# A decoder layer on one core: first B and A operands of the second MLP product loaded earlier, their order pinned, operands placed alike

## The chip, the cores and the metric

One core of a Trainium2 chip runs the whole kernel. The metric is the device time in microseconds (us), median of the runs; lower is better.

## What is computed

One decoder layer for a sequence of 1024 tokens and width 1024, float32 in and out. What matters here is its last part:

```python
x = x + gt1[:, None, :] * (merged @ w_out[l])
h2 = _modulate(x, norm2_g[l], sh2, sc2)
ff_out = jnp.square(jax.nn.relu(h2 @ w_ff1[l])) @ w_ff2[l]
x = x + gt2[:, None, :] * ff_out
...
return _rmsnorm(x, final_g)
```

`w_ff1` is 1024 x 4096 and `w_ff2` 4096 x 1024. Ahead of it stand a token mixing of two branches (a delta-rule recurrence and an attention with a forget gate), their gates and the projection `w_out`.

## The kernel before

Every float32 product is made of three products of rounded halves: an operand is cast to a high part on ACT, and DVE subtracts that from the operand to give the low part. Both MLP products are cut in 2 x 2 blocks and done in Strassen's way, with 7 block products instead of 8: some operands are sums of blocks (S1 to S4 on one side, T1 to T4 on the other).

**The way up** (`w_ff1`) runs over 16 pairs of column tiles. A pair has 7 products of 12 matmuls, each 128x512, in PSUM banks x, y and z. Its results, the A operands of the way down, are written to DRAM (`f_d`) by POOL's queue (`f_put`). In the last pair the first step of the way down is already mixed between the products, with operands that were loaded ahead (da and db, line 1405).

**The way down** (`w_ff2`) has 4 groups of 7 steps, given by the list `STEPS`; a step is 48 matmuls (line 1221) and sums up in the banks x or y. The steps of group 0 are numbered 0 to 6 in the text. A step needs two operands:

- the A operand dA: 1 MB from `f_d` on SP's queue (`load_a`, line 1503), ACT's two casts to dh (`hi_halves`, line 1410), DVE's two subtractions to fl (line 1591);
- the B operand: a raw block of 1 MB (`load_b`, line 1509), scaled by gt2 on DVE (`scale_b`, line 1517), for some steps a sum T of blocks (lines 1527 to 1536), then `split`: ACT's cast to wh (line 1099) and DVE's subtraction to wl (line 1100).

Step 0 takes A12 and B21, step 1 A11 and B11, step 2 S1 and T1 (from B12 and B11), step 3 S2 and T2 (from B22 and T1). After a step, the banks are added to acc by DVE (lines 1553 and 1559) or copied by ACT (line 1557).

**What sets the order.** Each engine runs its instructions in order, and so does SP with its loads. The order in which they stand is made by the framework's scheduler from the program and its estimates of time; the kernel writes the steps, and the scheduler moves instructions between them. A tile with a tag has a fixed number of buffers, so a new tile waits until the last reader of the old one is done: dA1 to dA27 take turns in the tags ar0, ar1 and dr, B21 lies in ur. B11_0 and B12_0 and the tiles of dA1 and dA2 lie where operands of the way up lay, so that a load into them waits for the last product with those.

Of the kernel before, what the change touches and what calls it, by code (L numbers as in the profile page):

```python
# [2 lines left out]

# [5 lines left out]
F32 = mybir.dt.float32  # L9
# [26 lines left out]
def build(ctx, tc, A, out):  # L36
# [6 lines left out]
    def pool(**kw):  # L43
        if kw.get("space") != bass.MemoryType.DRAM:
            kw["reuse_waits"] = "tile"
        return tc.tile_pool(**kw)
# [10 lines left out]
    def psum_pools(**banks):  # L57
        ppx.close()
        pools.clear()
        for tag, (n, size) in banks.items():  # L60
            pools[tag] = ppx.enter_context(pool(name=f"ps_{tag}", bufs=n, space=PSUM)), size

    def big(name, tag="pp"):
        return pools[tag][0].tile([P, pools[tag][1]], F32, tag=tag, name=name)
# [944 lines left out]
    gt2 = dpp.tile([P, D], F32, name="gt2")  # L1009
    sc2 = dpp.tile([P, KT], F32, name="sc2")  # L1010
    sh2 = dpp.tile([P, KT], F32, name="sh2")

    def ada_rest(gp):
        for j, dst in ((2, gt1), (5, gt2), (4, sc2), (3, sh2)):
# [82 lines left out]

    def split(hi, lo, src):
        ACT.copy(hi, src)  # L1099
        DVE.tensor_tensor(lo, src, f32(hi), ALU.subtract)  # L1100

    raw1, first, sums, rest = {}, {}, {}, {}

# [49 lines left out]
    ssq = px.tile([P, 8], F32, name="ssq2")  # L1153
    rs2 = px.tile([P, 8], F32, name="rs2")
    rtmp2 = px.tile([P, 16], F32, name="rtmp2")
    x1s = []

    def turn(t0, k, tag):
# [245 lines left out]
            nx[x] = dpr.tile([P, 4, 512], F32, name=f"d{x}0", tag=tag, bufs=1)  # L1404
            SP.dma_start(nx[x], src)

    def hi_halves(s, src):
        hs = [wp.tile([P, 2, 512], F32R, name=f"dh{s}_{i}", tag=("whi", "wlo")[s % 2], bufs=2) for i in range(2)]
        for i in range(2):
            ACT.copy(hs[i], src[:, 2 * i : 2 * i + 2])  # L1410
        return hs
# [14 lines left out]
    for j in range(2, NPAIR):  # L1426
# [33 lines left out]
        if not last:  # L1460
            rest_split(j + 1, "A22")
            first_first(j + 1)
            first_out(j + 1, 1)
    for name in ("S1", "S2", "S4"):
        f_sum(NPAIR - 1, name)
    for stack in (hx[2], hx[0], dax, hx[1], mix):
        stack.close()


    psum_pools(x=(4, 512), y=(4, 512))  # L1470
    with pool(name="fr", bufs=1, side="right") as fr, pool(name="fp", bufs=1) as fp:
        raws = {"B21": nx["b"]}
        acc = []
        ssq = fp.tile([P, 16], F32, name="ssq3")
        rs3 = fp.tile([P, 8], F32, name="rs3")
        rtmp = fp.tile([P, 16], F32, name="rtmp3")
        x1ts = {}

        STEPS = [
            ("y", True, "A12", "B21", [(0, 0)]),  # L1480
            ("x", True, "A11", "B11", [(0, 0)]),
            ("y", True, "S1", "T1", [(1, 1)]),
            ("x", False, "S2", "T2", [(0, 1)]),
            ("y", False, "S4", "B22", [(0, 1)]),
            ("x", False, "S3", "T3", [(1, 1)]),
            ("x", False, "A22", "T4", [(1, 0)]),
        ]
        flat = [(g, i) for g in range(NG) for i in range(7)]
        A_, ops, banks = {}, {}, {}

        def new_a(s):
            x = (s - 1) % 3
            A_[s] = (fr if x < 2 else dpr).tile([P, 4, 512], F32, name=f"dA{s}", tag=("ar0", "ar1", "dr")[x], bufs=1)

        def new_b(g, name):
            to, tag = {"B11": (fr, "B11"), "B12": (fr, "B12"), "B21": (dpr, "ur"), "B22": (fp, "B22")}[name]
            raws[name] = to.tile([P, 4, 512], F32, name=f"{name}_{g}", tag=tag, bufs=1)

        def load_a(s):
            g, i = flat[s]  # L1500
            if s > 2:
                new_a(s)
            SP.dma_start(A_[s], f_d[AOPS.index(STEPS[i][2]), 4 * g : 4 * g + 4].rearrange("j p n -> p j n"))

        def load_b(g, name):
            n, d = {"B11": (0, 0), "B12": (0, 1), "B21": (1, 0), "B22": (1, 1)}[name]
            if g or name not in ("B11", "B12"):
                new_b(g, name)
            SP.dma_start(raws[name], ff2[:, 8 * g : 8 * g + 8].rearrange("p (j i) n -> p j i n", i=2)[:, :, n, 512 * d : 512 * d + 512])

        new_a(2)
        new_b(0, "B12")
        new_a(1)
        new_b(0, "B11")

        def scale_b(name):
            DVE.tensor_tensor(raws[name], raws[name], by_gt2(int(name[2]) - 1), ALU.mult)

        def down_b(g, i):

            R = raws
            if i == 1:
                scale_b("B11")
            elif i == 2:
                scale_b("B12")
                R["T"] = fp.tile([P, 4, 512], F32, name=f"T_{g}", tag="T", bufs=1)
                DVE.tensor_tensor(R["T"], R["B12"], R["B11"], ALU.subtract)
            elif i == 3:
                scale_b("B22")
                DVE.tensor_tensor(R["T"], R["B22"], R["T"], ALU.subtract)  # L1530
            elif i == 5:
                DVE.tensor_tensor(R["B12"], R["B22"], R["B12"], ALU.subtract)
            elif i == 6:
                if g == 0:
                    scale_b("B21")
                DVE.tensor_tensor(R["T"], R["B21"], R["T"], ALU.subtract)
            elif i == 0:
                scale_b("B21")
            src = R[("B21", "B11", "T", "T", "B22", "B12", "T")[i]]
            if g == 0 and i == 1:  # L1540
                fr.tile([P, D], F32, name="fr_rest")
            h_, l_ = [to.tile([P, 4, 512], F32R, name=f"w{x}{g}_{i}", tag=f"w{x}", bufs=2) for x, to in (("h", fr), ("l", fp))]
            split(h_, l_, src)
            return [(h_[:, j], l_[:, j]) for j in range(4)]

        seen = set()

        def evict(o, t, d, scaled):
            sl = slice(512 * d, 512 * d + 512)
            if t >= len(acc):  # L1550
                acc.extend(fp.tile([P, D], F32, name=f"acc{t_}") for t_ in range(len(acc), t + 1))
            if (t, d) in seen:
                DVE.tensor_tensor(acc[t][:, sl], o, acc[t][:, sl], ALU.add)
            else:
                seen.add((t, d))
                if scaled:
                    ACT.copy(acc[t][:, sl], o)
                else:
                    DVE.tensor_tensor(acc[t][:, sl], o, gt2[:, sl], ALU.mult)
# [22 lines left out]
        def prepare(s):  # L1582
            if s >= len(flat):
                return
            g, i = flat[s]
            src = A_.pop(s)
            hs = hi_halves(s, src)
            fl = fp.tile([P, 4, 512], F32R, name=f"fl{s}", tag="fl", bufs=2)
            for i_ in range(2):
                sl = slice(2 * i_, 2 * i_ + 2)  # L1590
                DVE.tensor_tensor(fl[:, sl], src[:, sl], f32(hs[i_]), ALU.subtract)  # L1591
            ops[s] = [(hs[j // 2][:, j % 2], fl[:, j]) for j in range(4)], down_b(g, i)

        def loads(s):

            if s >= len(flat):
                return
            g, i = flat[s]
            load_a(s)
            if i in BL:  # L1600
                load_b(g, BL[i])

        ops[0] = nx["A"], nx["B"]
        loads(1)
        loads(2)
        for s, (g, i) in enumerate(flat):
            loads(s + 3)
            prepare(s + 1)
            if i == 5 and g + 1 < NG:
                load_b(g + 1, "B21")  # L1610
            if g == NG - 1 and i == 0:
                fg = dpp.tile([P, D], F32, name="fg", tag="gt1", bufs=1)
                POOL.dma_start(fg, A["final_g"].rearrange("(o n) -> o n", o=1).broadcast_to([P, D]))
            tag, opens, _, _, to = STEPS[i]
            fa, wb = ops.pop(s)
            for t in range(4):
                ts_ = slice(t * P, t * P + P)
                if opens:
                    banks[tag, t] = bank(f"{tag}{g}_{i}_{t}", tag)
                o = banks[tag, t]  # L1620
                for j in range(4):
                    (fh, fl), (wh, wl) = fa[j], wb[j]
                    mmx(o, fh[:, ts_], wh, opens and j == 0, False)
                    mmx(o, fl[:, ts_], wh, False, False)
                    mmx(o, fh[:, ts_], wl, False, j == 3)
                for half, d in to:
                    evict(o, t + 4 * half, d, s > 0)
                if g == NG - 1:
                    if i == 1:
                        square(t, 0)  # L1630
                    elif i == 4:
                        square(t, 1)
                        finish(t)
                    elif i == 5:
                        square(t + 4, 1)
                    elif i == 6:
                        square(t + 4, 0)
                        finish(t + 4)
            if g in (1, 2) and i >= 3:
                residual(4 * (g - 1) + i - 3)  # L1640

# [22 lines left out]
```

## Time and profile before

| | |
|---|---|
| median of 3 runs | 1678.47 us (1678.31 to 1679.96) |
| the profiled execution, its own time | 1680.21 us |
| its span in the trace | 1678.5 us |
| mean granted TensorE clock | 0.991 |
| busy: PE, DVE, ACT, POOL | 95%, 67%, 44%, 21% of the span |
| way up (first x product to last A22) | about 1022 to 1351 us |
| way down, step 1 to the last product | 1369.54 to 1661.4 us |

Times in the trace are counted from the span's start. A matmul's duration in the trace is longer than the spacing of two, since they overlap; the pace is read from start to start, or from a piece of the chain of so many matmuls.

### The profile page before, as it was taken

Reading aid. Unit: us, or ns where it says so; the run is one execution under the profiler, and the core shown is the slowest. Engines: PE = TensorE matmul, PEld = TensorE weight load, DVE = VectorE, ACT = ScalarE, POOL = GpSimd, SP = SyncE. Lnnn points to the kernel's source line nnn. Section 1 sums busy time; section 2 is a strip of 40 time slices with the busy share of each in tenths; the row PEclk is TensorE's granted clock in tenths of the full one; section 3 lists DMA queues with packets and bytes.
Section 4 is the critical chain, followed back from the end, with each engine's and each line's share of the span. In section 5 each row is a group of like instructions: output and inputs, shape, how many; then the busy total and the mean of one; then the engine's idle time right before and its main releaser. Section 6 shows DMA issues by size and latency. Waiting matters only on the chain.

```text
span 1678.5 us, 21911 instructions
## 1 busy us (share of the span) xinstructions
PE 1591.5 (95%) x8293; PEld 1274.8 (76%) x8293; DVE 1132.0 (67%) x1685; ACT 730.7 (44%) x1138; POOL 357.9 (21%) x362
## 2 busy tenths in 40 slices
PE   2989999999999999999999999999999979999997
PEld 1767777777777878888887787777777858888886
DVE  5777665657655736665737656975555579899978
ACT  5455343535454623332333234655545534433334
POOL 4310000899990011221110000122211110000000
PEclk9999999999999999999999999999999989999999
DMA  8525456422223178778767431344444474364422
GB/s 242 149 79 161 127 152 155 113 63 63 70 60 117 32 213 262 231 242 230 239 207 237 152 113 51 139 150 154 144 160 150 158 288 161 120 220 158 168 75 101
DMA packets 217111, 256.24 MB, mean 153 GB/s; under 512 B 30097, under 2 KB 156330, under 8 KB 216878
## 3 DMA queue, kind: packets, MB, share of 16 engines
q1 hardware_dynamic: 204094, 209.99, 41.3%
q0 software_dynamic: 12704, 44.57, 6.9%
q8 instruction: 65, 1.06, 0.3%
q14 instruction: 40, 0.33, 0.1%
q10 hardware_dynamic: 208, 0.28, 0.0%
HBM read 178.16 MB, written 72.45 MB: 149 GB/s over the span
## 4 chain that ended last, share of the span: by engine, by line
PE 70%; DVE 10%; DMA 7%; ACT 5%; issue 3%; SPq 0%; DVEq 0%; ACTq 0%
PE x L1221 18%; PE y L1221 11%; PE p_gb L41 5%; PE p_out L41 5%; PE p_ga L41 3%; PE p_ob L41 2%; PE p_fv L41 2%; DMA ur<-in_w_ff 2%; PE my L41 2%; PE p_fk L41 2%; PE p_fq L41 2%; PE z L1221 2%; PE p_v L41 2%; PE yv L41 2%; PE tp L825 2%
## 5 line engine op out<-in xcount | busy, mean ns | idle before, releaser
L1410 ACT CAST dh<-dA 128x1024 fp32r<-128x1024 f32 x54 | 56.4, 1046 | 139.9 <-PE x L1221 72.2
L1221 PE MATMUL x<-wh,dh 128*128 128x512 f32 x256 | 102.1, 399 | 9.4 <-ACT wh L1099 9.4
L645 POOL TENSOR_TENSOR dg<-dg,inv 128x62 f32<-128x62 f32 (+30 forms) x62 | 100.2, 1616 | 4.8
L1221 PE MATMUL x<-wl,dh 128*128 128x512 f32 x256 | 100.9, 395 | 0.0
L1221 PE MATMUL x<-wh,fl 128*128 128x512 f32 x256 | 100.1, 391 | 0.0
L644 POOL TENSOR_TENSOR inv<-dg 128x62 f32<-128x62 f32 (+30 forms) x62 | 92.8, 1497 | 4.9
L1591 DVE TENSOR_TENSOR fl<-dA,dh 128x1024 fp32r<-128x1024 f32 x54 | 65.1, 1218 | 16.1 <-ACT dh L1410 10.3
L1221 PE MATMUL y<-wh,dh 128*128 128x512 f32 x176 | 69.4, 394 | 0.0
L1221 PE MATMUL y<-wl,dh 128*128 128x512 f32 x176 | 68.6, 393 | 0.5 <-DVE wl L1100 0.5
L1221 PE MATMUL y<-wh,fl 128*128 128x512 f32 x176 | 68.3, 388 | 0.0
L829 DVE TENSOR_TENSOR pl<-tp,ph 128x512 fp32r<-128x512 f32 (+1 forms) x80 | 49.1, 631 | 24.9 <-ACT ph L828 24.6
L1221 PEld LDWEIGHTS x<-wh,dh 128*128 128x128 f32 x256 | 48.8, 191 | 19.6 <-ACT wh L1099 9.8
L885 DVE CUSTOM_DVE_ANT_0 pt<-s,cb 128x512 f32<-128x512 f32 (+2 forms) x64 | 36.4, 584 | 37.5 <-PE s L41 36.6
L887 ACT ACTIVATE pt<-pt,sm 128x128 f32<-128x128 f32 (+3 forms) x64 | 49.5, 775 | 24.4 <-DVE sm L885 23.4
L707 POOL TENSOR_TENSOR sw<-sbd,wcs 64x256 f32<-64x256 f32 x28 | 22.9, 816 | 167.9 <-DVE sbd L708 137.7
L1245 ACT ACTIVATE ff<-ff 128x512 f32<-128x512 f32 x48 | 30.3, 632 | 64.9 <-DVE ff L1331 29.5
L1221 PEld LDWEIGHTS x<-wl,dh 128*128 128x128 f32 x256 | 48.3, 189 | 12.0 <-DVE wl L1100 0.5
L1221 PEld LDWEIGHTS x<-wh,fl 128*128 128x128 f32 x256 | 48.6, 190 | 10.7
L828 ACT CAST ph<-tp 128x512 fp32r<-128x512 f32 (+1 forms) x80 | 41.6, 543 | 29.1 <-PE tp L825 27.2
L1236 POOL DMA_DIRECT2D f_d<-ff x48 | 25.9, 540 | 125.5 <-ACT ff L1246 121.1
L825 PE MATMUL tp<-ident,pt 128*128 128x128 f32 x288 | 49.6, 282 | 2.1 <-ACT pt L887 1.7
L41 PE MATMUL p_out<-h_wo,hhi 128*128 128x512 f32 x128 | 50.8, 397 | 0.6 <-ACT h_wo L1056 0.6
(586 smaller groups left out, 4932.6 us busy)
## 6 DMA issues: line engine op xcount, KB each, us to landing
dA<-f_d SPq DMA_DIRECT2D x27, 1024.0 KB
aw<-in_w_ada SPq DMA_DIRECT2D x32, 512.0 KB
ur<-in_w_ff SPq DMA_DIRECT2D x30, 512.0 KB
B<-in_w_ff SPq DMA_DIRECT2D x15, 1024.0 KB
f_d<-ff POOLq DMA_DIRECT2D x48, 256.0 KB, 4.3
wa<-in_w_ada SPq DMA_DIRECT2D x16, 512.0 KB
sc_d<-scb SPq DMA_DIRECT2D x16, 512.0 KB
sct<-sc_d SPq DMA_DIRECT2D x16, 512.0 KB
```

Source lines behind the costliest of these rows:

```text
L41: PE.matmul(o, l, r, start=start, stop=stop)
L644: POOL.tensor_tensor(tv, dg[:, 0:s, s : s + 1].broadcast_to([P, s, m]), dg[:, s : s + 1, s + 1 :].broadcast_to([P, s, m]), ALU.mult)
L645: POOL.tensor_tensor(dg[:, 0:s, s + 1 :], dg[:, 0:s, s + 1 :], tv, ALU.add)
L825: PE.transpose(tp[:, x * P : (x + 1) * P], pr[b][:, t * P : (t + 1) * P], ident)
L828: ACT.copy(ph[:, 0:w_], tp[:, 0:w_])
L829: DVE.tensor_tensor(pl[:, 0:w_], tp[:, 0:w_], ph[:, 0:w_].bitcast(F32), ALU.subtract)
L885: DVE.tensor_tensor_reduce(pt[:, c0:c1], sv, cb[:, c0:c1], -0.125, low, ALU.add, ALU.min, st_[:, x : x + 1])
L887: ACT.activation(pt[:, 0:n], pt[:, 0:n], AF.Exp, bias=low, scale=-1.0, accum_out=ls[:, b : b + 1])
L1221: PE.matmul(o, l, r, start=start, stop=stop, skip_group_check=True)
L1245: ACT.activation(f, f, AF.Relu)
L1410: ACT.copy(hs[i], src[:, 2 * i : 2 * i + 2])
L1591: DVE.tensor_tensor(fl[:, sl], src[:, sl], f32(hs[i_]), ALU.subtract)
```

## The change

It does three things.

1. *Early loads.* The code that makes the first tiles of the way down now stands ahead of the last sums of the last pair. SP loads B11 and dA1 right behind db, and DVE scales B11 at once. Step 1's high parts get buffers of their own (`wh_second`; `dh_second`, which lies in the tag dr, where dA3 lay), so that they can be made before step 0 is over. The loads of steps 1 to 3 are kept in the order in which they are written (`in_order`).
2. *Order of evictions.* `behind(done)` lets what is written under it be issued only after the last instruction in a list: the last f sums behind B11's scaling, step 0's later evictions and the preparing of steps 2 to 6 behind the low parts made before them.
3. *Three unused tiles*, `dpp_rest` (64 bytes in each partition), `px_rest` (384) and `fp_rest` (352). Nothing reads or writes them. They move what is allocated after them: before, hhi, hlo, dh and the halves of ur began at an offset of 352 within 512 bytes, S1 to S4, T1, T4, wh and h_wo0 to h_wo3 at 416, h_wo4 to h_wo7 at 480, wl and fl at 0; after the change all of these begin at 352.

```diff
+    def behind(done):
+
+        return tc.issue_after(done[-1].ins) if done else nullcontext()
...
+    dpp.tile([P, 16], F32, name="dpp_rest")
...
+    px.tile([P, 96], F32, name="px_rest")
...
-    def hi_halves(s, src):
-        hs = [wp.tile([P, 2, 512], F32R, name=f"dh{s}_{i}", tag=("whi", "wlo")[s % 2], bufs=2) for i in range(2)]
+    def hi_halves(s, src, second=False):
+        if second:
+            h = dpr.tile([P, 4, 512], F32R, name="dh_second", tag="dr", bufs=1)
+            hs = [h[:, 2 * i : 2 * i + 2] for i in range(2)]
+        else:
+            hs = [wp.tile([P, 2, 512], F32R, name=f"dh{s}_{i}", tag=("whi", "wlo")[s % 2], bufs=2) for i in range(2)]
...
+    def in_order(load, yes):
+        if yes:
+            tc.keep_in_program_order(load)
...
+    new_a(2)
+    new_b(0, "B12")
+    new_a(1)
+    new_b(0, "B11")
+    load_b(0, "B11")
+    load_a(1)
+    early = [scale_b("B11")]
+    with behind(early):
+        for name in ("S1", "S2", "S4"):
+            f_sum(NPAIR - 1, name)
...
+        fp.tile([P, 88], F32, name="fp_rest")
...
             if i == 1:
-                scale_b("B11")
+                if g:
+                    scale_b("B11")
...
-            h_, l_ = [to.tile([P, 4, 512], F32R, name=f"w{x}{g}_{i}", tag=f"w{x}", bufs=2) for x, to in (("h", fr), ("l", fp))]
-            split(h_, l_, src)
+            if g == 0 and i == 1:
+                h_ = fq.tile([P, 4, 512], F32R, name="wh_second")
+            else:
+                h_ = fr.tile([P, 4, 512], F32R, name=f"wh{g}_{i}", tag="wh", bufs=2)
+            l_ = fp.tile([P, 4, 512], F32R, name=f"wl{g}_{i}", tag="wl", bufs=2)
+            early.append(split(h_, l_, src))
...
+            if i in BL and s == 3:
+                load_b(g, BL[i])
             load_a(s)
-            if i in BL:
+            if i in BL and s != 3:
                 load_b(g, BL[i])
...
         ops[0] = nx["A"], nx["B"]
-        loads(1)
         loads(2)
         for s, (g, i) in enumerate(flat):
-            loads(s + 3)
-            prepare(s + 1)
+            if s:
+                loads(s + 3)
+            with behind(early if 0 < s < 6 else []):
+                prepare(s + 1)
...
-                for half, d in to:
-                    evict(o, t + 4 * half, d, s > 0)
+                with behind(early if s == 0 and t else []):
+                    for half, d in to:
+                        evict(o, t + 4 * half, d, s > 0)
...
+            if s == 0:
+                loads(3)
```

Two engines' rows show what moves. In the names, dA and B carry a buffer's number and not the step's. First SP's loads, from db on. Before, dA_11639 is dA3, B_0_11641 is B22, dA_11633 dA1, B_0_11634 B11, dA_11631 dA2 and B_0_11632 B12:

```order
L1405 DMA db_11488<-in_w_ff 128x4x512
L1503 DMA dA_11639<-f_d 128x4x512
L1509 DMA B_0_11641<-in_w_ff 128x4x512
L1503 DMA dA_11633<-f_d 128x4x512
L1509 DMA B_0_11634<-in_w_ff 128x4x512
L1503 DMA dA_11631<-f_d 128x4x512
L1509 DMA B_0_11632<-in_w_ff 128x4x512
L1503 DMA dA_11716<-f_d 128x4x512
L1503 DMA dA_11788<-f_d 128x4x512
```

After, B_0_11611 is B11, dA_11610 dA1, dA_11608 dA2, B_0_11609 B12, B_0_11718 B22, dA_11722 dA4, dA_11794 dA5 and dA_11720 dA3:

```order
L1411 DMA db_11490<-in_w_ff 128x4x512
L1514 DMA B_0_11611<-in_w_ff 128x4x512
L1508 DMA dA_11610<-f_d 128x4x512
L1508 DMA dA_11608<-f_d 128x4x512
L1514 DMA B_0_11609<-in_w_ff 128x4x512
L1514 DMA B_0_11718<-in_w_ff 128x4x512
L1508 DMA dA_11722<-f_d 128x4x512
L1508 DMA dA_11794<-f_d 128x4x512
L1508 DMA dA_11720<-f_d 128x4x512
```

B11 and dA1 came fourth and fifth among the rows from db on and are now the first two behind it. dA3, which came first, now comes last, behind dA4 and dA5. The wait that goes with B11's load is for the last product of the way up that reads T1l; the one with dA3's is for the last matmul of step 1, which reads dh_second.

Then DVE, from the last dl of db to the first evictions of step 0 and what makes step 1's operands. Before:

```order
L1331 TENSOR_TENSOR ff_15_11522<-y_11490,ff_15_11522 128x512
L1421 TENSOR_TENSOR dl_11569<-db_11488,dh_0_11573 128x512
L1517 TENSOR_TENSOR db_11488<-db_11488,gt_5349 128x2048
L1321 TENSOR_TENSOR ff_15_11503<-x_11469,ff_15_11503 128x512
...
L1559 TENSOR_TENSOR acc_11714<-y_0_3_11701,gt_5349 128x512
L1517 TENSOR_TENSOR B_0_11641<-B_0_11641,gt_5349 128x2048
L1591 TENSOR_TENSOR fl_11647<-dA_11633,dh_0_11643 128x1024
L1591 TENSOR_TENSOR fl_11647<-dA_11633,dh_1_11644 128x1024
L1517 TENSOR_TENSOR B_0_11634<-B_0_11634,gt_5349 128x2048
L1100 TENSOR_TENSOR wl_1_11653<-B_0_11634,wh_1_11652 128x2048
```

And after the change:

```order
L1431 TENSOR_TENSOR dl_11571<-db_11490,dh_0_11575 128x512
L1351 TENSOR_TENSOR fs_11583<-ff_15_11442,ff_15_11524 128x512
L1327 TENSOR_TENSOR ff_15_11505<-x_11471,ff_15_11505 128x512
L1517 TENSOR_TENSOR B_0_11611<-B_0_11611,gt_5349 128x2048
...
L1105 TENSOR_TENSOR wl_1_11655<-B_0_11611,wh_second 128x2048
L1622 TENSOR_TENSOR fl_11650<-dA_11610,dh_second 128x1024 x2
L1590 TENSOR_TENSOR acc_11671<-y_0_0_11658,gt_5349 128x512
L1590 TENSOR_TENSOR acc_11686<-y_0_1_11673,gt_5349 128x512
```

The scaling of db (as B21) has left this place for the time of step 6's operand. B11's scaling, wl and fl of step 1 stood behind the evictions of step 0 and now stand ahead of them, with f sums of the last pair between.

One more place, DVE between step 1's evictions and step 3's low part, after the change (T_11732 is T, x_1_3 the last bank of step 1):

```order
L1584 TENSOR_TENSOR acc_11716<-x_1_3_11780,acc_11716 128x512
L1105 TENSOR_TENSOR wl_2_11735<-T_11732,wh_2_11734 128x2048
L1517 TENSOR_TENSOR B_0_11718<-B_0_11718,gt_5349 128x2048
L1622 TENSOR_TENSOR fl_11800<-dA_11720,dh_0_11796 128x1024
L1622 TENSOR_TENSOR fl_11800<-dA_11720,dh_1_11797 128x1024
L1556 TENSOR_TENSOR T_11732<-B_0_11718,T_11732 128x2048
L1517 TENSOR_TENSOR B_1_12002<-B_1_12002,gt_5349 128x2048
L1105 TENSOR_TENSOR wl_3_11806<-T_11732,wh_3_11805 128x2048
```

Before, wl of step 2 stood ahead of the last of these evictions; now it stands behind it. The scaling of B22 (B_0_11718) was the first thing behind step 0's evictions and is now here.

## Rows read from the trace of the kernel before

**Rows 1.** The page's first part: busy time of each engine, share, instructions.
```profile
PE 1591.5 (95%) x8293; PEld 1274.8 (76%) x8293; DVE 1132.0 (67%) x1685; ACT 730.7 (44%) x1138; POOL 357.9 (21%) x362
```

**Rows 2.** Windows around the seam: PE, PEld, DVE, ACT, POOL busy; PEclk, DMA share, GB/s.
```profile
1350.00:1360.00 10.00, 10.00 (x44) 7.89 (x42) 3.67 (x6) 2.32 (x4) 3.63 (x7) 1.00 1.01 370
1360.00:1370.00 10.00, 0.62 (x2) 0.46 (x2) 7.84 (x6) 3.42 (x3) 0.55 (x1) 0.68 1.04 401
1370.00:1380.00 10.00, 10.00 (x36) 7.62 (x36) 9.68 (x7) 2.27 (x3) 0.00 (x0) 0.81 0.31 119
```

**Rows 3.** Chain that ended last, at the seam: start us, us, what.
```profile
1333.79 6.38 DMA db<-in_w_ff
...
1340.20 2.00 ACT dh L1410 x2
...
1351.34 8.83 PE y L1221 x38
...
1360.80 2.28 DVE B L1517
1363.08 2.27 DVE fl L1591 x2
1365.35 2.21 DVE B L1517
...
1367.59 1.91 ACT wh L1099
...
1369.54 10.71 PE x L1221 x36
...
1380.28 0.69 DVE acc L1553
...
1383.17 2.21 DVE wl L1100
...
1385.42 9.51 PE y L1221 x40
1394.93 11.05 PE x L1221 x48
1405.98 10.99 PE y L1221 x48
```

**Rows 4.** Timeline of PE, step 1: start us, us, operation, count [idle before <-releaser].
```profile
1369.54 0.80 PE L1221 MATMUL x<-wh,dh 128*128 128x512 f32 x1 [9.38 <-ACT wh L1099]
...
1373.31 0.63 PE L1221 MATMUL x<-wl,dh 128*128 128x512 f32 x1
1373.74 0.44 PE L1221 MATMUL x<-wh,dh 128*128 128x512 f32 x1
```

**Rows 5.** Timeline of PE, the last product of the way up with T1l.
```profile
1337.00 0.39 PE L1221 MATMUL y<-T1l,S1h 128*128 128x512 f32 x1
```

**Rows 6.** Timeline of SP's queue: B11's load and a later one (B21 of group 1).
```profile
1346.56 0.51 SPq L1509 DMA_DIRECT2D B<-in_w_ff  x1
...
1398.43 0.37 SPq L1509 DMA_DIRECT2D B<-in_w_ff  x1
```

**Rows 7.** Timeline of DVE: the scaling that waited for that later load.
```profile
1403.38 2.29 DVE L1517 TENSOR_TENSOR B<-B,gt 128x2048 f32<-128x2048 f32 x1 [1.64 <-DMA B<-in_w_ff]
```

**Rows 8.** Chain elsewhere, long pieces of 128x512 matmuls: gates, w_out, a pair's z.
```profile
367.37 10.89 PE p_ga L41 x48
940.76 32.88 PE p_out L41 x141
1206.79 2.75 PE z L1221 x12
```

**Rows 9.** Chain in the way up: ur's load in two pairs that follow each other.
```profile
1214.82 6.67 DMA ur<-in_w_ff
1234.59 6.63 DMA ur<-in_w_ff
```

More of the change, by code (lines that the diff above doesn't have):

```diff
@@ L1 @@
 import math
-from contextlib import ExitStack
+from contextlib import ExitStack, nullcontext
 import concourse.bass as bass
@@ L1099, in split @@
         ACT.copy(hi, src)
-        DVE.tensor_tensor(lo, src, f32(hi), ALU.subtract)
+        return DVE.tensor_tensor(lo, src, f32(hi), ALU.subtract)
     raw1, first, sums, rest = {}, {}, {}, {}
@@ L1463, in build, with new_a, new_b, load_a @@
             first_out(j + 1, 1)
-    for name in ("S1", "S2", "S4"):
-        f_sum(NPAIR - 1, name)
-    for stack in (hx[2], hx[0], dax, hx[1], mix):
+    for stack in (hx[2], hx[0], dax):
+        stack.close()
+    STEPS = [
+        ("y", True, "A12", "B21", [(0, 0)]),
+        ("x", True, "A11", "B11", [(0, 0)]),
+        ("y", True, "S1", "T1", [(1, 1)]),
+        ("x", False, "S2", "T2", [(0, 1)]),
+        ("y", False, "S4", "B22", [(0, 1)]),
+        ("x", False, "S3", "T3", [(1, 1)]),
+        ("x", False, "A22", "T4", [(1, 0)]),
+    ]
+    flat = [(g, i) for g in range(NG) for i in range(7)]
+    fr = ctx.enter_context(pool(name="fr", bufs=1, side="right"))
+    fp = None
+    raws, A_ = {"B21": nx["b"]}, {}
+    def new_a(s):
+        x = (s - 1) % 3
+        A_[s] = (fr if x < 2 else dpr).tile([P, 4, 512], F32, name=f"dA{s}", tag=("ar0", "ar1", "dr")[x], bufs=1)
+    def new_b(g, name):
+        to, tag = {"B11": (fr, "B11"), "B12": (fr, "B12"), "B21": (dpr, "ur"), "B22": (fp, "B22")}[name]
+        raws[name] = to.tile([P, 4, 512], F32, name=f"{name}_{g}", tag=tag, bufs=1)
+    def in_order(load, yes):
+        if yes:
+            tc.keep_in_program_order(load)
+    def load_a(s):
+        g, i = flat[s]
+        if s > 2:
+            new_a(s)
+        in_order(SP.dma_start(A_[s], f_d[AOPS.index(STEPS[i][2]), 4 * g : 4 * g + 4].rearrange("j p n -> p j n")), s < 4)
+    def load_b(g, name):
+        n, d = {"B11": (0, 0), "B12": (0, 1), "B21": (1, 0), "B22": (1, 1)}[name]
+        if g or name not in ("B11", "B12"):
+            new_b(g, name)
+        in_order(SP.dma_start(raws[name], ff2[:, 8 * g : 8 * g + 8].rearrange("p (j i) n -> p j i n", i=2)[:, :, n, 512 * d : 512 * d + 512]), g == 0)
+    def scale_b(name):
+        return DVE.tensor_tensor(raws[name], raws[name], by_gt2(int(name[2]) - 1), ALU.mult)
+    new_a(2)
[8 more added lines that the diff above has]
+            f_sum(NPAIR - 1, name)
+    for stack in (hx[1], mix):
         stack.close()
     psum_pools(x=(4, 512), y=(4, 512))
-    with pool(name="fr", bufs=1, side="right") as fr, pool(name="fp", bufs=1) as fp:
-        raws = {"B21": nx["b"]}
+    with pool(name="fp", bufs=1) as fp, ExitStack() as sq_:
         acc = []
@@ L1476, in build @@
         rtmp = fp.tile([P, 16], F32, name="rtmp3")
+        fp.tile([P, 88], F32, name="fp_rest")
         x1ts = {}
[L1479 to L1517, printed above, removed]
+        ops, banks = {}, {}
+        fp.tile([P, 4, 512], F32, name="B22_0", tag="B22", bufs=1)
         def down_b(g, i):
@@ L1541, in down_b @@
                 fr.tile([P, D], F32, name="fr_rest")
-            h_, l_ = [to.tile([P, 4, 512], F32R, name=f"w{x}{g}_{i}", tag=f"w{x}", bufs=2) for x, to in (("h", fr), ("l", fp))]
-            split(h_, l_, src)
+            if g == 0 and i == 1:
[4 more added lines that the diff above has]
+            early.append(split(h_, l_, src))
             return [(h_[:, j], l_[:, j]) for j in range(4)]
         seen = set()
+        fq = sq_.enter_context(pool(name="fq", bufs=1))
         def evict(o, t, d, scaled):
@@ L1586, in prepare @@
             src = A_.pop(s)
-            hs = hi_halves(s, src)
+            hs = hi_halves(s, src, s == 1)
             fl = fp.tile([P, 4, 512], F32R, name=f"fl{s}", tag="fl", bufs=2)
```

## Prediction

> **What bounds the kernel now.** I read the page first: TensorE's row [rows 1] says 95% busy, so only its idle stretches or the pace of its products can give time back. The windows around the seam come second. In [rows 2] PE is full in 1350 to 1360, has 0.62 us of work in 1360 to 1370, and is full again in 1370 to 1380 at a granted clock of 0.81, against 1.00 before; the same rows show the DMA engines at a share of 1.01 and 1.04 with 370 and 401 GB/s just where PE stands still, and DVE 9.68 us busy right after. Third, the chain that ended last [rows 3]: read it as a list of who made PE wait. PE y ends at 1360.17 (step 0), then come DVE's scaling of a B block, two fl, another scaling, ACT's wh, and PE only again at 1369.54. The B scaled first, at 1360.80, is B22, which step 1 doesn't read (it stands first in the vector queue); the one at 1365.35 is B11, which step 1 does read. Fourth, PE's own list [rows 4]: 9.38 us idle, released by wh; the matmuls at 1373.31 and 1373.74 are 0.43 us apart, about twice the usual spacing, so the engine still ran at 1.2 GHz, the lower of its two levels, after that idle stretch.
>
> **What the stall is worth.** A step of the way down is 48 matmuls. An undisturbed one takes 10.99 us, as the pieces at 1394.93 and 1405.98 show with 11.05 and 10.99 [rows 3]. Without any wait step 3 would start at 1360.2 + 2 x 10.99 = 1382.2; it starts at 1394.93. So **12.7 us** are lost: 9.4 of waiting, and 3.3 within the two steps, of which 0.5 is the wait for wl that ends at 1385.42 and the rest is the slow clock and the refill. All of it stands on the path: from 1394.93 to the last product the chain has nothing but PE.
>
> **Part 1, the early loads.** B11's load now stands on SP right behind db's and waits for the last T1l product of the up phase. The list has that product at 1337.00 [rows 5], so it is issued at about 1337.4 instead of 1346.56 [rows 6], and dA1's behind it. A 1 MB load takes from 4.95 us (issued 1398.43, its reader released at 1403.38 [rows 6, 7]) to 6.38 us (db, the chain's 1333.79 [rows 3]). Sharing with the rest of db, I put B11 at 1344 and dA1 one megabyte later: 1 MB at the 401 GB/s of [rows 2] is 2.6 us, so 1346.6. DVE's scaling (2.2 us) follows ff, which the removal of db's scaling pulls to about 1346.7: done by 1349. wh_second has its own buffer and needs no old reader: ACT is taken by the A22 activations until about 1351.1, then wh_second (1.91) to 1353.0 and dh_second (2.00) to 1355.0; wl by 1355.2, fl (2.27) by 1357.5. Step 0 ends at 1360.2, so everything for step 1 is there **2.7 us before** it is wanted, and the wait and the slow clock go. Were B11 to land 4.95 or 6.38 us after 1337.4 makes no difference; the cover is gone only if it lands after about 1346.7 + 2.7.
>
> **Part 2, what is late next.** Step 1 then runs 1360.2 to 1371.2. DVE has acc of step 0 to 1360.9, fl2 (dh2 still waits for step 0's end: 1362.2) to 1363.4, B12's scaling to 1365.6, one acc, T to 1368.4; ACT's wh_2 to 1370.3. DVE's next acc (0.69 us) waits for the last matmul of step 1 at 1371.2, and wl_2 stands behind it: 1371.9 to 1374.1. PE can run 8 matmuls of step 2 without wl_2 (40 of 48 follow the wait in [rows 3]), so it waits from 1373.0 to 1374.1: **1.1 us**, where 0.5 was. Step 2 ends at 1383.3. dA3 now goes into the tile that held dh_second, so SP sends it only when the last matmul of step 1 is done, and behind dA4 and dA5; those wait for fl1 and fl2 and are long out. Landing: 1371.2 + 4.95 to 6.38. By the short value dh3 ends 1378.3, fl3 1379.6, T 1381.7, wh_3 1383.6: a wait of 0.3, then wl_3 behind B11's scaling of the next group, 1386.1, against 1385.4: 0.7. By the long value 1.4 more. I take the short one, since its row also is a load in the way down with little beside it, plus 0.3: **2.4 us** of new waits, with ends 0.5 (DVE finds gaps) and 3.5. The seam gives 12.7 - 2.4 = **10.3 us** (9.2 to 12.2). B21's scaling and its T move later, to step 6's turn, where DVE has room; the count of instructions on SP is the same.
>
> **Part 3, the three unused tiles.** They cost no instruction. They move all of PE's operands to offset 352 within 512 bytes, where before wh, S and T1 stood at 416, some of h_wo at 480, wl and fl at 0. Which rows price that? Streams that stood alike before: p_ga 48 in 10.89 us, 226.9 ns each; z 12 in 2.75, 229.2 [rows 8]. Streams that did not: p_out 141 in 32.88, 233.2 [rows 8]; the way down 10.99 for 48, 229.0 [rows 3]. So alike is cheaper or equal.
> - The way down: between 0 (z's pace) and 28 x 48 x 2.1 ns = 2.8 us (p_ga's). I take 1.0, about the lower third, because the z row, of the same kind of product, is no faster than the down steps.
> - w_out: some 300 matmuls on PE's path, 0 to 300 x 6.3 ns = 1.9. I take 0.9.
> - The way up: 84 matmuls a pair could gain 84 x 4 ns = 0.34 us, but a pair's time is set by a loop: ur's load at 1214.82 and the next at 1234.59, 19.77 apart [rows 9], while PE's 84 at 231 ns are 19.4. Only A22's own 12 matmuls lie in the loop: 0.05 a pair, about 0.1 to 0.8 in all; I take 0.1.
>
> Together **2.0 us**, ends 0 and 5.5.
>
> The Trainium skill, page "SBUF — State Buffer", section "Who interferes with whom", speaks against this part: TensorE has read ports of its own for the moving operand and for the weights, and nothing but the pair shared by VectorE and GpSimd contends. By that rule the term would be 0 and the sum 10.3; the trace's 226.9 against 233.2 ns doesn't look like it, though the two streams differ in more than their place.
>
> **The sum.** 10.3 + 2.0 = 12.3 us. The profiled execution took 1680.21, 1.74 above the median of 1678.47; against its own time the change gives 1667.9, against the median **1666.2**, which is my forecast. Some 0.2% (3.4 us) is what a measurement here can tell from no change.
>
> **Rivals.**
> - *Placement does nothing.* For it: z at 229.2 and the down steps at 229.0 are one pace. Then 1678.47 - 10.3 = 1668.2. It is also what that section on SBUF gives.
> - *Placement pays fully.* All streams go to p_ga's 226.9: 1678.47 - 10.3 - 5.5 = 1662.7. For it: p_out and p_ga are the same kind of product. Against: z.
> - *The wait moves to dA3.* DVE was busy 9.68 of 10 us after the seam and the new order leaves it no idle stretch; with a late dA3 (6.38 us or more) and B11, db and dA1 sharing the DMA engines at 1337 (db 1.4 us late delays dh, dl, and all behind it, since the chain runs through db [rows 3]), the seam gives 9.2 - 1.4 = 7.8, with no gain from placement: 1670.7.
> - *The end on the other side: 352 is the slow place.* If the common offset makes weights and moving data collide, the 2,900 matmuls of w_out, up and down all pay. Place: PE's pace. Price: 2.9 us for each ns. It eats the seam's 10.3 from 3.6 ns on, and ends slower by over 3.4 us from 4.7 ns on; at the spread that the rows show, 6.3 ns, it is 1678.5 - 10.3 + 18.3 = 1686.5. Against: p_ga, alike at 352, has the best pace in the trace.
> - *It doesn't do what it says.* If B11's load were held as before, by memory or by a late reader, step 1 would wait as now: 1678.5, the same. Against: the only wait on it is the T1l product.
>
> **Chances.** Forecast (1664.5 to 1668) 0.50; placement nothing 0.22; fully 0.11; the wait at dA3 0.10; not what it says 0.04; slow place 0.03. The first four are all faster by over 0.2%: 0.93; same 0.04; slower 0.03. The range goes from 1662.0, a little beyond full placement, to 1671.0, a little beyond the dA3 case; it leaves out the last two cases and the tails.
>
> **What would show it.** Right: PE's idle before step 1 gone from 9.38 to under 0.5, no slice of PE clock below 1.00 at the seam, B11's issue on SP at 1337 to 1338, DVE's wait list with wl for step 2 and ACT's wh for step 3, 1 us each or so; down steps at 10.92 to 10.99; ur's period still 19.7. Wrong: a wait on B11's scaling ahead of the f sums on DVE, dh_0 of db later than 1342, a wait of over 2 us at step 3, or down steps above 11.0.

## The result, and the profile after

The changed kernel takes **1665.85 us**, median of 6 runs (1661.92 to 1672.53), against 1679.22 of the kernel before, measured beside it (1677.92 to 1682.08): a ratio of 0.9912, 95% interval 0.9891 to 0.9933. That is 13.4 us between the medians; 1666.2 was forecast. The profiled execution is the slowest of the six, 1672.53 us with a span of 1670.8; two more profiles of the same kernel (below) have spans of 1667.6 and 1662.4.

The chain at the seam, of the changed kernel (start us, us, what), answers to [rows 3]:

```profile
1335.01 6.44 DMA db<-in_w_ff
...
1348.72 3.06 PE x L1227 x12
1351.78 9.80 PE y L1227 x43
1361.58 10.89 PE x L1227 x48
...
1372.49 6.65 DMA dA<-f_d
...
1379.16 1.06 ACT dh L1420
...
1380.24 2.36 DVE fl L1622 x2
1382.60 2.21 DVE T L1556
...
1384.84 1.91 ACT wh L1104
...
1386.79 13.00 PE x L1227 x48
1399.79 10.88 PE y L1227 x48
```

The first PE piece is A22's products. Between the end of step 0 (PE y, 1361.58) and step 1 (PE x, 48 matmuls) nothing stands any more: no scaling of B, no wh. But there is a new piece: at the end of step 1 the load of dA3 begins, and dh, fl, T and wh of step 3 hang on it one behind the other. Step 3 takes 13.00 us instead of 10.88. The windows answer to [rows 2] (PE, PEld, DVE, ACT, POOL busy; PEclk, DMA share, GB/s):

```profile
1360.00:1370.00 10.00, 10.00 (x45) 8.26 (x45) 9.65 (x10) 2.50 (x3) 1.10 (x2) 1.00 1.04 405
1370.00:1380.00 10.00, 8.83 (x39) 6.98 (x38) 5.87 (x5) 2.37 (x2) 0.00 (x0) 1.00 0.88 309
1380.00:1390.00 10.00, 8.02 (x32) 5.80 (x31) 9.76 (x6) 7.29 (x10) 0.00 (x0) 0.92 0.36 114
```

PE is full in 1360 to 1370 at a clock of 1.00, where it had 0.62 us of work at 0.68. What is lost now is lost 10 to 20 us later, in 1370 to 1390: there PE has 16.85 us of 20, and in the second half the clock is at 0.92. PE's own list in that place, answering to [rows 4] (start us, us, operation, count [idle before <-releaser]):

```profile
1386.79 0.50 PE L1227 MATMUL x<-wh,dh 128*128 128x512 f32 x1 [1.99 <-ACT wh L1104]
...
1390.28 0.63 PE L1227 MATMUL x<-wh,fl 128*128 128x512 f32 x1
1390.71 0.63 PE L1227 MATMUL x<-wl,dh 128*128 128x512 f32 x1
```

The idle stretch before step 1 was 9.38 us; the one before step 3 is 1.99 us. The matmuls at 1390.28 and 1390.71 are 0.43 us apart, so the engine fell to 1.2 GHz here too, some 2 us into the step. SP's list shows the early load (issue, us, line):

```profile
1338.59 0.37 SPq L1514 DMA_DIRECT2D B<-in_w_ff  x1
1339.05 12.90 SPq L1508 DMA_DIRECT2D dA<-f_d  x2
```

B11 is issued 3.6 us behind db instead of 12.8 us [rows 3, 6]. Far from the seam, pieces of the chain in w_out and at the end of the way down:

```profile
990.42 35.16 PE p_out L41 x155
...
1640.14 13.61 PE x L1227 x60
```

Before, the same two pieces are:

```profile
986.02 35.84 PE p_out L41 x155
...
1647.69 13.75 PE x L1221 x60
```

The w_out piece of 155 matmuls, 35.84 us before, is 226.8 ns a matmul now; the last product ends at 1640.14 + 13.61 = 1653.75 instead of 1661.44, and behind it 17.05 us are left, as before (17.06).

**One measure for what follows.** Profiles of one and the same kernel differ by up to 8 us in when the last A22 products start (1348.72, 1348.49 and 1340.88 in three of the changed kernel). So the tables below measure from there: *seam*, from the start of A22's products to the end of step 3, and *rest*, from there to the end of the last product. Without any wait or slow clock the seam would be 3.06 + 9.80 + 3 x 10.88 = 45.5 us, by the pieces above. In the kernel before, A22's products are this piece of the chain, ahead of the 38 matmuls of step 0 in [rows 3]:

```profile
1348.31 3.04 PE x L1221 x12
```

So the two kernels' seams don't hold the same work: before, 38 matmuls of step 0 stand behind A22's products, now 43. The five, some 1.1 us, count against the change in this column; the part on the prediction comes back to it.

| kernel (profile) | A22 starts | seam | rest |
|---|---|---|---|
| before, first and second profile | 1348.31, 1344.53 | 57.7, 57.3 | 255.5, 255.5 |
| changed, three profiles | 1348.72, 1348.49, 1340.88 | 51.1, 49.0, 50.8 | 254.0, 253.0, 253.7 |
| e2: change without the unused tiles | 1344.98 | 49.3 | 255.5 |
| e3: unused tiles alone | 1345.00 | 56.7 | 253.0 |
| e4: dA3 in its own place | 1339.21 | 51.7 | 253.0 |
| e5: dA3's place and two orders | 1346.88 | 48.0 | 253.0 |
| e6: wl of step 2 first | 1347.51 | 49.8 | 253.0 |
| e7: without `behind` | 1345.37 | 55.3 | 253.1 |
| e8: without dh_second | 1342.39 | 51.9 | 253.4 |
| e9: four orders and dA3's place | 1345.64 | 46.2 | 253.0 |
| e10: without fp_rest | 1344.68 | 49.2 | 260.4 |

### The profile page after: what moved, and what is told of

It is laid out like the page before. It is cut to its first block, busy times and chain, and to the rows that moved or that the text cites. A ratio compares the mean times of both kernels' runs of the same rounds, so it can differ in the third digit from the quotient of the medians.

```text
span 1670.8 us, 21904 instructions
## 1 busy us (share of the span) xinstructions
PE 1586.6 (95%) x8293; PEld 1277.5 (76%) x8293; DVE 1132.8 (68%) x1685; ACT 730.7 (44%) x1138; POOL 357.9 (21%) x362
## 4 chain that ended last, share of the span: by engine, by line
PE 60%; DVE 13%; DMA 11%; ACT 6%; issue 4%; SPq 0%; DVEq 0%; ACTq 0%
PE x L1227 13%; PE y L1227 7%; DMA ur<-in_w_ff 5%; PE p_gb L41 5%; PE p_out L41 5%; PE p_ga L41 3%; PE my L41 2%; PE p_ob L41 2%; PE p_fv L41 2%; PE p_fk L41 2%; PE p_fq L41 2%; PE p_v L41 2%; PE yv L41 2%; PE tp L829 2%; PE s L41 1%
## 5 line engine op out<-in xcount | busy, mean ns | idle before, releaser
L1227 PE MATMUL x<-wh,dh 128*128 128x512 f32 x240 | 94.3, 393 | 2.7 <-ACT wh L1104 2.0
L1227 PE MATMUL x<-wh,fl 128*128 128x512 f32 x240 | 94.0, 392 | 0.0
L1227 PE MATMUL x<-wl,dh 128*128 128x512 f32 x240 | 93.5, 392 | 0.0
L833 DVE TENSOR_TENSOR pl<-tp,ph 128x512 fp32r<-128x512 f32 (+1 forms) x80 | 49.2, 632 | 24.9 <-ACT ph L832 24.6
L1227 PEld LDWEIGHTS x<-wh,dh 128*128 128x128 f32 x240 | 45.3, 189 | 12.9 <-ACT wh L1104 2.4
L41 PE MATMUL p_gb<-hhi,wl_gb 128*128 128x512 f32 x128 | 51.4, 401 | 0.0
```

What stands on the lines that cost most here:

```text
L41: PE.matmul(o, l, r, start=start, stop=stop)
L833: DVE.tensor_tensor(pl[:, 0:w_], tp[:, 0:w_], ph[:, 0:w_].bitcast(F32), ALU.subtract)
L1227: PE.matmul(o, l, r, start=start, stop=stop, skip_group_check=True)
```

## Experiments

**The changed kernel again** (e1 and e11), with no edit.

> The changed kernel once more, for a second profile. Theory: the time falls into the same scatter as before (1662 to 1673 us), and a profile shows every step from 4 on at 10.88 us and a wait of 1 to 2.5 us for ACT's wh ahead of step 3; a faster run is one in which the stretch between 865 and 945 us, where PE waits for loads of m, is shorter, not one in which the seam differs. Rival: the scatter sits in the seam (dA3's landing and the slow clock that follows), so that a faster run has no wait at step 3.

> The changed kernel a third time, beside the two others of this call. Expected: 1662 to 1670 us, A22's start to the end of step 3 at 49 to 51 us with a wait at steps 2 and 3, and 253.0 us from there to the last product.

Measured: 1664.01 us (1663.15 to 1669.28), ratio 0.9922 [0.9908, 0.9936], and 1664.67 (1661.99 to 1666.06), ratio 0.9910 [0.9896, 0.9925]. The result holds. The seam of e1 (chain):

```profile
1334.81 6.42 DMA db<-in_w_ff
...
1348.49 3.01 PE x L1227 x12
...
1372.22 5.82 DMA dA<-f_d
...
1385.83 2.29 DVE wl L1105
1388.17 9.36 PE x L1227 x40
1397.53 10.88 PE y L1227 x48
```

dA3's load took 5.82 us here against 6.65, PE waited 1.2 us for wh and 0.4 for wl, the clock did not fall, and the seam is 2.0 us shorter than in the first profile. So both theory and rival hold a part: a wait stays at step 3 in each profile, it differs with dA3's landing, but most of the scatter lies ahead of A22, in the second column of the table. A part of that is where the theory put it: from the last products of p_ob to the first long piece of w_out, where PE waits for loads of m, the chain takes 77.0 us in the first profile (867.2 to 944.2), 73.5 in e1 and 72.4 in e11 (864.3 to 936.7). Of the 7.8 us between the first and the third that is 4.6; 2.9 lie still further ahead. The seam of e11 is nearly that of the first profile, with a slow step 3:

```profile
1327.24 6.37 DMA db<-in_w_ff
...
1364.64 6.57 DMA dA<-f_d
...
1378.86 12.78 PE x L1227 x48
```

**The two halves of the change apart** (e2, e3). The rows of every engine stand in the same order as in the kernel each is taken from.

```diff
 e2, on the changed kernel; e3 adds the same three lines to the kernel before
-    dpp.tile([P, 16], F32, name="dpp_rest")
-    px.tile([P, 96], F32, name="px_rest")
-        fp.tile([P, 88], F32, name="fp_rest")
```

> The change without its three unused tiles: every engine's rows stand in the same order, only the places of the operands are those of before. Theory (the pace per matmul depends on the place): down steps go back from 10.88 to 10.99 us, 28 x 0.11 = 3.1 us, and w_out and the way up give back some 0.5 to 2, so 3.5 to 5 us slower than the changed kernel, 8.5 to 10 faster than before. Rival (place does nothing, the 10.88 came with the new order): steps stay at 10.88 and the time equals the changed kernel's.

> The kernel before with the three unused tiles alone, rows in the same order. Theory: down steps at 10.88 us, 3 to 4 us faster than before; in the way up the 12-matmul pieces go from 2.80 to 2.72 us, but the pair's period stays at 19.7 and PE waits ahead of A22 in most pairs, so that nothing more comes of it. Rival A: nothing changes. Rival B: the way up gains as well, 84 x 5 ns x 15 = 6 us more.

Measured: e2 1666.56 us (1665.25 to 1668.75), ratio 0.9932 [0.9920, 0.9944]; e3 1673.38 (1670.48 to 1674.92), ratio 0.9968 [0.9956, 0.9979]. Each half is faster than the kernel before by itself. The table says where: e2 has the seam of the changed kernel and the rest of the kernel before, e3 the other way round. e2's gain over the kernel before was larger than expected (11.7 us between the medians, where 8.5 to 10 stood), and its loss against the changed kernel measured beside it smaller (2.6, where 3.5 to 5 stood); e3's gain is 4.9 (3 to 4 expected). The two gains add up to 16.5 us, 2.3 more than both changes together gave there, so a single median carries some 2 us that isn't explained. Does the place pay in the way up? The waits of PE for the sum that A22 needs, in 1020 to 1340, before and in e3 (line waited for: us in total, times, longest):

```profile
PE x L1221 <- DVE ff L1321: 0.8, 1, 0.8
```

```profile
PE x L1223 <- DVE ff L1323: 5.1, 11, 0.8
```

The products there became faster (12 in 2.73 us in the chain of the changed kernel, 2.80 before) and PE waits that much longer ahead of A22, in 11 pairs instead of one. The pair's period stays: ur's loads follow each other at 1212.32 and 1232.17 in e3, 19.85 us, against 19.77 [rows 9].

**One place alone put back** (e10): fp_rest is left out, so that wl, fl and wh_second begin at 0 within 512 bytes, and wh, dh stay at 352.

```diff
-        fp.tile([P, 88], F32, name="fp_rest")
```

> The changed kernel without fp_rest alone: wl, fl and wh_second begin at 0 within 512 bytes, all other operands stay at 352. Theory (it is the place of an operand against the one that is loaded or streamed beside it that counts): two of three matmuls of a down step still meet an operand at 0, so a step takes 10.93 to 11.0 us, and step 4 to the last product 254 to 255.5 us against 253.0. Rival (the 416 of wh was what was slow): a step stays at 10.88.

Measured: 1671.46 us (1667.84 to 1673.01), ratio 0.9946 [0.9929, 0.9963], 6.8 us slower than the changed kernel measured beside it. The chain's last steps in e10:

```profile
1629.04 11.20 PE y L1227 x48
1640.24 14.01 PE x L1227 x60
```

A step takes 11.20 us, 233.3 ns a matmul, not between 10.88 and 10.99 but beyond both. No instruction differs from the changed kernel's. So the place where tiles begin does set PE's pace, and a mixed placement can cost more than that of the kernel before. (fp_rest moves all that lies behind it; of PE's operands these are wl, fl and wh_second.)

**dA3 in a place of its own** (e4). It lies where acc6 and acc7 will lie, and its load needn't wait for step 1's end.

```diff
+        if s == 3:
+            A_[s] = fp.tile([P, 4, 512], F32, name="dA3", tag="a67", bufs=1)
+            return
...
+            if t == 6 and len(acc) == 6:
+                a67 = fp.tile([P, 2, D], F32, name="acc67", tag="a67", bufs=1)
+                acc.extend(a67[:, i_] for i_ in range(2))
```

> The changed kernel, but dA3 lies where acc6 and acc7 will lie and no longer waits for dh_second's last reader. Theory (dA3's late issue makes the 2.0 us wait at step 3, and that wait the slow clock in it, 13.00 us for a step in place of 10.88): both go, 3.5 to 4.5 us faster than the changed kernel, about 1661.5 us; the wait of 1.2 us for wl at step 2 stays. Rival (DVE's queue is the bound at the seam): wh of step 3 comes no more than 1 us earlier, since T and the scaling ahead of it are as late as before, and the gain is under 1 us.

Measured: 1666.38 us (1662.64 to 1668.60), ratio 0.9926 [0.9914, 0.9938]; no gain, seam 51.7. Neither theory had it. ACT's list in e4 (start us, us, operation [idle before <-releaser]):

```profile
1352.07 1.06 ACT L1420 CAST dh<-dA 128x1024 fp32r<-128x1024 f32 x1 [0.32 <-PE y L1227]
1362.09 1.99 ACT L1420 CAST dh<-dA 128x1024 fp32r<-128x1024 f32 x2 [8.97 <-DMA dA<-f_d]
1363.99 1.89 ACT L1104 CAST wh<-T 128x2048 fp32r<-128x2048 f32 x1
```

The wait at step 3 is gone, and a new one of 3.0 us stands at step 2: the scheduler put dA3's casts ahead of step 2's wh, and ACT stood for 8.97 us at a cast whose load shared the DMA engines with others and took 11.07 us by the chain. T was ready at about 1360. The load was freed, and the order of a queue made it useless.

**The orders around it** (e5, e6, e9).

```diff
 e6 is the changed kernel with this line alone; e5 is e4 with all of this
-                with behind(early if s == 0 and t else []):
+                with behind(early if (s == 0 and t) or (s == 1 and t == 3) else []):
...
-        ACT.copy(hi, src)
+        casts.append(ACT.copy(hi, src))
...
-            hs = hi_halves(s, src, s == 1)
+            with behind(casts if s == 3 else []):
+                hs = hi_halves(s, src, s == 1)
 e9 is e5 with two more
-                    scale_b("B11")
+                    with behind(early[:4] if g == 1 else []):
+                        scale_b("B11")
...
-                        evict(o, t + 4 * half, d, s > 0)
+                        with behind(casts if s == 2 else []):
+                            evict(o, t + 4 * half, d, s > 0)
```

> The changed kernel with step 2's wl ahead of the last eviction of step 1, and nothing else of it. Theory (dA3's issue at the end of step 1 sets when step 3 can start): the 1.2 us wait at step 2 goes, and the wait for wh at step 3 grows by as much, from 1.2 to 2.0 up to 2.4 to 3.2; A22 to the end of step 3 stays at 49 to 51 us, no gain. Rival (the two waits are independent): 1.2 us less, 47.8 to 49.9.

> dA3 in its own place as in the run before, and two orders added: ACT casts step 3's dh only behind step 2's wh, and DVE makes step 2's wl ahead of the last eviction of step 1. Theory (in the run with dA3 alone the casts of dA3 stood ahead of wh_2 on ACT and held it for a load that shared the DMA engines; dA3's landing and these two places in the queues are all that is left of the stall): from the start of A22's products to the end of step 3 it takes 45.5 to 46.5 us, against 49.0 and 51.1 in the two profiles of the changed kernel, PE waits less than 0.5 us in all at steps 1 to 3, and the time is 3 to 5 us below the changed kernel's, 1660 to 1662 us. Rival (DVE is the bound there, 97% busy): a wait of 2 us or more stays at step 3, whatever the order.

> The run with dA3's own place and two orders, and two more: step 3's wh stands ahead of step 2's copies on ACT, and step 3's wl ahead of the scaling of the next group's B11 on DVE, which waited for its load. Theory (in that run 1.6 us were left at step 3 since wl_3 stood behind a scaling that waited for a load, so the stall that is left is a matter of queue order): PE waits under 0.5 us in all at steps 1 to 3, A22's start to the end of step 3 takes 45.5 to 46.4 us against 48.0, and the time is 1.5 us less than in that run, about 1660 us, 4 to 6 below the changed kernel in the same call. Rival (DVE at 93% of 1370 to 1380 is the bound): over 1 us of waiting stays.

e6: 1667.07 us (1663.89 to 1669.11), ratio 0.9927 [0.9905, 0.9950]; the wait at step 2 is gone and that at step 3 is 2.4 us:

```profile
PE x L1227 <- ACT wh L1104: 2.4, 1, 2.4
```

The seam is 49.8, within the changed kernel's own 49.0 to 51.1: a wait taken away ahead of the real bound comes back in front of it. That bound is dA3's issue.

e5: 1661.39 us (1660.91 to 1666.64), ratio 0.9906 [0.9887, 0.9924]. The seam is 48.0 and not 46. PE waits 1.6 us for wl at step 3, because of this on DVE:

```profile
1380.91 2.29 DVE L1522 TENSOR_TENSOR B<-B,gt 128x2048 f32<-128x2048 f32 x1 [1.53 <-DMA B<-in_w_ff]
1383.12 2.29 DVE L1107 TENSOR_TENSOR wl<-T,wh 128x2048 fp32r<-128x2048 f32 x1
```

DVE stood idle for 1.53 us at the scaling of the next group's B11, whose load had not landed, with wl_3 behind it. So DVE isn't the bound there; it is a queue once more.

e9: 1662.58 us (1660.04 to 1663.61), ratio 0.9896 [0.9880, 0.9912]. Its seam is 46.2 us, 0.7 above the one without waits, and at steps 1 to 3 PE waits only this:

```profile
PE x L1229 <- DVE wl L1107: 0.2, 1, 0.2
```

The seam behaves as the theory says. In the time the two are not that far apart: 2.1 us below the changed kernel measured beside it (4 to 6 expected), with intervals that overlap, where the seams of the profiles differ by 4.5. e9 is the fastest version by the ratio, and by the profile the one with nothing left at the seam; that it beats the changed kernel in time is likely, not settled.

**Without the pinned evictions** (e7).

```diff
-        return tc.issue_after(done[-1].ins) if done else nullcontext()
+        return nullcontext()
```

> The changed kernel without its pinned evictions (behind does nothing): B11's load stays early, but DVE's B11 scaling, wl and fl of step 1 go back behind step 0's evictions. Theory (the order on DVE made the stall, not the load): PE waits 4 to 5.5 us at step 1, for one eviction, B11's scaling and wh, half of the 9.4 of before (no B22 scaling and no fl ahead), and the clock falls again; 4 to 6 us slower than the changed kernel. Rival (the load was what was late): no wait at step 1, and the time equals the changed kernel's.

Measured: 1670.21 us (1666.06 to 1675.94), ratio 0.9956 [0.9941, 0.9971]; seam 55.3. The wait at step 1 is back, a little longer than the 4 to 5.5 us expected, though B11 and dA1 are loaded as early as in the changed kernel:

```profile
PE x L1227 <- ACT dh_second L1420: 5.9, 1, 5.9
```

An eviction, B11's scaling (2.21 us) and ACT's casts follow step 0 again, and the clock in 1360 to 1370 is 0.52. Of what the seam gains, some 2 us come without the pins; the rest needs the order. The reverse, an order without the early loads, has no run: in the kernel before, B11 was issued at 1346.56 [rows 6], and its scaling at 1365.35 stood behind another scaling and two fl, 4.55 us [rows 3]. How much of the gain the order alone would give isn't shown.

**Without dh_second** (e8): dA1's high parts go into the usual tiles, dA3 has the tag dr.

```diff
-            hs = hi_halves(s, src, s == 1)
+            hs = hi_halves(s, src)
```

> The changed kernel, but dA1's high parts go into the usual tiles, which are free only at the end of step 0, and dA3 has the tag dr to itself. Theory: step 1 waits 1 to 2.5 us for dh and fl instead of step 3 for dA3; A22 to the end of step 3 takes 48 to 50 us, about the changed kernel's. Rival: the casts after step 0 cost as much as before (fl behind evictions, slow clock), 53 us or more.

Measured: 1666.85 us (1666.13 to 1667.63), ratio 0.9932 [0.9915, 0.9949]; seam 51.9. That is above the theory's 48 to 50 and below the rival's 53, and it came by another way than either. Step 1 ran without a wait to speak of (48 matmuls in 11.11 us): the first of the usual tiles came free at 1353.64 in ACT's list, ahead of step 0's end at 1355.20, so its cast was early enough. Step 2 waited, for a wh that stood on ACT behind dA3's casts, which wait here for step 1's products to free their tiles. It also waited 1.6 us for wh at step 3. PE's list:

```profile
1369.24 0.50 PE L1227 MATMUL y<-wh,dh 128*128 128x512 f32 x1 [2.94 <-ACT wh L1104]
```

**The kernel before, profiled again** (e12).

> The kernel before, profiled once more, to see how much of the stretch ahead of the seam is scatter. Theory: the start of A22's last products, 1348.3 in the first profile, falls anywhere in 1342 to 1350, as in the profiles of the other kernels (1339 to 1349), with A22's start to the end of step 3 at 57.7 and from there to the last product 255.5 us again. Rival (the unused tiles also gain ahead of the seam): it stays at 1348 or later.

1676.04 us in its single run. The seam and the rest repeat to within 0.4 us, and A22 starts 3.8 us earlier than in the first profile:

```profile
1330.01 6.39 DMA db<-in_w_ff
...
1344.53 3.01 PE x L1221 x12
1347.54 8.83 PE y L1221 x38
...
1401.83 10.99 PE y L1221 x48
```

## Why the prediction was right, and where its terms were not

The forecast of 12.3 us met a measured 13.4 through two errors of opposite sign; that they nearly cancel is luck.

- **Part 1, the early loads: right.** "The wait and the slow clock go": PE's 9.38 us are gone and the windows show 1.00. B11's scaling starts at 1348.58 in the changed kernel's list of DVE with no idle time before it, as the sum had it. The cover was there: fl of step 1 ends at 1359.48 in that list, 2.1 us ahead of step 0's end (2.7 forecast). e7 shows that it takes the order on DVE to use it.
- **Part 2, what is late next: right in kind, too small.** It named both new waits, for wl at step 2 (1.1 us; measured 1.2) and at step 3 behind dA3. The step that failed is "I take the short one": dA3's load takes 6.65, 5.82 and 6.57 us in the three profiles, not 4.95. Why it differs isn't shown: B11 of the next group is issued right behind it in all three, but also in e2 and e10, where it takes 5.51. And the prediction left out that such a wait can bring the slow clock back: in two of the three profiles step 3 itself takes 12.78 and 13.00 us. So the seam still loses 5.6, 3.5 and 5.3 us against 45.5, 4.8 in the mean, where 2.4 (at most 3.5) stood. The loss before was right: 57.7 and 57.3 against 3.04 + 8.83 + 3 x 10.99 = 44.8, or 12.7. The table's seams differ by only 57.5 - 50.3 = 7.2 us, because of the five matmuls that now stand behind A22's products. From the start of db's load to the end of step 3, which holds them on both sides, it takes 72.2 and 71.8 us before and 64.8, 62.7 and 64.4 with the change: 8.0 less, of which 0.4 is the place of the operands in its steps. So waits and clock give **about 7.6 and not 10.3**.
- **Part 3, the place: right in sign, too small.** The down steps went to p_ga's pace, 10.88 for 48 or 226.7 ns, not to z's: 2.5 us in the rest where nothing waits there (1.5 and 1.8 in the two profiles where a load of the next group let PE wait 0.7 and 0.4 us for an eviction), and 0.4 in the seam, where 1.0 was taken. The step that failed is the choice of the z row as a guide. w_out gave 0.7 on its second piece and 0.6 on its first where the clock held (32.29 for 141 in e3 against 32.88), 1.3 against 0.9; in the first profile of the changed kernel that piece took 33.89, at a clock of 0.70 in 945 to 950. The way up gave nothing, as said, and by the mechanism that was named: e3's waits. Together **about 4 and not 2.0**.
- Some 7.6 + 4.2 = 11.8 us are found in the profiles. The medians differ by 13.4, and by 14 and 15.5 in the two repeats. The rest lies in the scatter ahead of A22, where single profiles can't tell a gain of 2 us; that stays open.
- **The rivals.** "Placement does nothing" falls by e3 and e10: e10 and the changed kernel run the same rows at 11.20 and 10.88 us a step. The Trainium skill, page "SBUF — State Buffer", section "Who interferes with whom", has no contention outside the port pair shared by VectorE and GpSimd. Taken as the prediction took it, for a term of 0, the trace does not agree with it. "The wait moves to dA3" is what happened to the seam, and its 7.8 us is nearer to what was measured than the forecast's 10.3, though not by its own sum: db, which it put 1.4 us late, took 6.44 us against 6.38. The place's larger gain hid it in the time. "352 is the slow place" falls: it is the fastest seen. Another offset common to all operands wasn't tried, so whether they have to be alike or to be at 352 isn't shown.

## What to carry to other kernels

Where a chain of waits shows an engine at work on something that nobody waits for yet (here the scaling of B22 and the evictions), the gain lies in the order of that queue: the early loads without the pinned order were worth about 2 of 8 us. After such a change look for the next queue in which a late load stands ahead of ready work; four of them followed each other here (dA3 in its reused buffer, dh_3 ahead of wh_2, a scaling ahead of wl_3, copies ahead of wh_3), and removing one of them alone moved the wait and gave nothing (e4, e6). Check where the operands of the long product streams begin: with all of them at one offset within 512 bytes (352) the steps of the way down ran at 226.7 ns a matmul, with mixed offsets at 229 to 233.

## What was not expected of the hardware

- A pace that hangs on addresses alone: 10.88, 10.99 and 11.20 us for the same 48 matmuls, with all operands at 352; with wh at 416, dh at 352 and wl, fl at 0; and with wh, dh at 352 and wl, fl at 0. Why the last is the slowest isn't settled. Nor is this: the tiles of the z products did not move, and yet their pace went from 229.2 [rows 8] to 226.7 ns (12 in 2.72 us in the changed kernel's chain). And T1 and S1 stood alike at 416 before, but their 12 matmuls took 2.77 us (1334.46 to 1337.23 in PE's list), 230.8 ns each. So the offset of a product's own operands is not the whole of it; why it matters, no run here shows.
- An idle stretch does not fix the clock by its length. After 1.99 us the clock fell in the changed kernel, after 1.2 us in e1 it did not. After 2.4 us in e6 it fell again, but after 2.94 us in e8 it did not. Step 3 of e6 (chain), and the windows of e8:

```profile
1384.53 12.79 PE x L1227 x48
```

```profile
1360.00:1370.00 10.00, 7.07 (x31) 5.56 (x30) 9.57 (x9) 3.90 (x3) 0.00 (x0) 1.00 1.04 392
1370.00:1380.00 10.00, 9.78 (x43) 7.76 (x42) 10.00 (x6) 2.12 (x4) 0.00 (x0) 1.00 0.56 176
```

- dA3's load of 1 MB took 5.5 to 6.7 us where it was issued at the end of step 1, with B11's behind it. It took 11.07 us in e4, where it was issued at 1350.99 among others; there the windows show a DMA share of 1.04 and 396 GB/s (1355 to 1365).
